# First layer of a two-layer decoder trunk: convolution over all 512 tokens at once, and Strassen's algorithm for nine of its FFN pairs

## The chip, the cores and the metric

The kernel runs on one core of one Trainium2 chip. The core has a matrix engine (TensorE, PE; its weight loads are listed as PEld), a vector engine (VectorE, DVE), a scalar engine (ScalarE, ACT), a general-purpose engine (GpSimd, POOL) and a queue that issues DMA transfers (SyncE, SP). Matmuls write PSUM, which has eight banks of 128 x 512 float32; all else lives in SBUF. The metric is the device time of one execution in microseconds (us).

## What is computed

Two layers over 512 tokens of width 1024, in float32. Layer 0 is a causal Conformer convolution followed by a SwiGLU FFN of hidden width 2816; layer 1 is sliding-window attention followed by another FFN. Only layer 0 and its neighbours matter here:

```python
def swiglu_ffn(x, w_up, w_down):
    gate, up = jnp.split(x @ w_up, 2, axis=-1)
    return (jax.nn.silu(gate) * up) @ w_down

def conformer_conv(x, w_pw1, b_pw1, w_dw, b_dw, ln_g, ln_b, w_pw2, b_pw2):
    a = jax.nn.glu(x @ w_pw1 + b_pw1, axis=-1)
    y = lax.conv_general_dilated(a, w_dw[:, None, :], window_strides=(1,),
        padding=((CONV_WIDTH - 1, 0),), feature_group_count=D_MODEL) + b_dw
    y = jax.nn.silu(layernorm(y, ln_g, ln_b))
    return y @ w_pw2 + b_pw2

# layer 0
h = h + conformer_conv(rmsnorm(h, norm_mix[0]), ...)
h = h + swiglu_ffn(rmsnorm(h, norm_ffn[0]), ffn_w_up[0], ffn_w_down[0])
# layer 1: K/V and queries from h, attention, output projection, FFN, final RMSNorm
```

The convolution is depthwise: each of 1024 channels has its own 31 taps along the tokens. The LayerNorm behind it runs over the channels, so it needs all channels of a token before any of them can go on.

## The kernel before

Activations are held transposed: channels on the 128 partitions, tokens along the free dimension, eight channel blocks (`KT`) of 128. `h` is the residual stream.

**Number formats on PE.** A float32 matmul (both operands float32) is recorded as two PE records. Most products instead split each operand into a high and a low part of a reduced format (float32r) and add three matmuls (`mm3`, L308 to L310); the split of a weight chunk is a cast on ACT (L249) and a subtraction on DVE (L250), done by `advance` some chunks ahead of use. Weights stream in chunks of 512 KB through one list, `PLAN`, by SP.

**Layer 0 is done in two halves of 256 tokens.** `Pw1` (line 778) is the first pointwise projection in float32, one channel block and half at a time, and `gate` makes the GLU into a padded row `a_pad`. `Half.taps` is the depthwise convolution of a block: `N_POOL` of the 31 taps are products on ACT (L817, L819) summed on POOL (L820); the others are multiply-adds on DVE into half a PSUM bank (L825, L827); POOL adds the two sums (L831). `conv` takes the blocks in pairs and alternates between the two. The LayerNorm statistics come from matmuls with an all-ones matrix of 128 x 128 over 256 columns (L876, L870), `scales_a` and `scales_b` make them into a mean and a scale per token, `spread` broadcasts these over the partitions with a matmul, and `rows` applies them with silu. `shift_rows` keeps the values small before they are squared.

The first half's convolution (`h0`) runs beside the 16 block-and-half projections. The second half's (`h1`) is a list of background steps (`job`) that `pace` hands out between weight chunks, while PE does `pw2` and the first part of the FFN for the first half: `pw2(h0.z)` in float32 (L306, `NATIVE`), then `ffn_part(0, 0, ..., HALF[0])` with five of the eleven FFN pairs at 256 columns. A pair is 256 hidden channels: `ffn_up` makes gate and up, `down_group` adds its part of the down product. Then the same for the second half, with the low part of a product fused behind the high part (`twin`, `mm2`, L340 and L341), reading the same weights from memory again. The other six pairs then run once over all 512 tokens (`ALL`).

**Layer 1's FFN** takes its first two pairs plainly at 512 columns, and the other nine by `ffn_prod`: one level of Strassen's algorithm, in which the product of a weight matrix cut in 2 x 2 blocks and an activation cut in 2 x 2 blocks takes seven block products in place of eight. The seven right factors are made once by `right_factors` in the background of the first part; the left ones are sums of weight blocks, made on DVE by `block` (L210 to L215) as the weights come in. The parts are `HALVES1` and `LAST`.

**Order.** Each engine takes its instructions in the order that the framework laid down when the kernel was built: instructions written earlier come first, but one that is not ready by the framework's own estimate is passed by a later one that is. `tc.issue_after` pins single instructions behind another. So the order in the code is a priority, not a promise.

Of the kernel before, what the change touches and what calls it, by code (L numbers as in the profile page):

```python
# [51 lines left out]
def chunk_plan():  # L52
# [7 lines left out]
    def ups(layer, lo, hi):  # L60
        for pair in range(lo, hi):
            if layer == 1 and pair >= PLAIN1:
                plan.extend(("prod", pair, j) for j in range(7))
# [11 lines left out]
    for _ in range(2):  # L75
        pw2()
        ffn(0, *HALVES0[0])
    ffn(0, *HALVES0[1])
# [20 lines left out]
NATIVE = {i for i in range(PLAN.index(("up", 0, 0, 0, 0)))}  # L99
CHUNKS = [("pw1", w * KT + ct) for ct in range(KT) for w in range(2)]  # L100
CHUNKS += [c for c in dict.fromkeys(PLAN) if c[0] != "prod"]
CHUNKS += [("up", 1, pair, half, which) for pair in range(PLAIN1, LAST[1]) for which in range(2) for half in range(2)]
# [3 lines left out]
def lay_weights(w):  # L106
# [3 lines left out]
    for i, c in enumerate(CHUNKS):  # L110
        if c[0] == "pw1":
            t = w["conv_w_pw1"][0][:, c[1] * P:(c[1] + 1) * P].reshape(KT, P, P)
# [44 lines left out]
def hybrid_trunk(ctx: ExitStack, tc: tile.TileContext, xT, W, prm_in, wdw_in, sinks, relb, onehot, fin, out):  # L157
# [35 lines left out]
    def load_block(i):  # L193
        _, pair, j = PLAN[i]
        if j == 0:
            four[pair] = str_pool[0].tile([P, 3, 1024], F32, tag="blocks", name=uid("blocks"))
        if j < 2:
            r = raws[i] = wpool.tile([P, 1024], F32, tag="raw", name=uid("raw"), bufs=4)
            nc.sync.dma_start(r, W[CHUNK_AT["up", 1, pair, j, 0]])
            nc.sync.dma_start(four[pair][:, j], W[CHUNK_AT["up", 1, pair, j, 1]])  # L200

    def block(i):

        _, pair, j = PLAN[i]
        b21, b22, s1 = (four[pair][:, n] for n in range(3))
# [29 lines left out]
    def advance():  # L235
        u = stream["use"]
        load(u + DMA_AHEAD)
        while stream["split"] < min(len(PLAN), u + SPLIT_AHEAD):
# [5 lines left out]
            if i in NATIVE:  # L244
                splits[i] = (r, None)
                continue
# [43 lines left out]
    def get(*key):  # L290
# [11 lines left out]
        return tuple(w and w.rearrange("p (a b) -> p a b", **sh) for w in (hi, lo))  # L302

    def mm3(out, w, x, start, stop, **kw):
        if w[1] is None:
            nc.tensor.matmul(out, w[0], x, start=start, stop=stop)  # L306
            return
# [4 lines left out]
    class Act:  # L312
        def __init__(self, n, w=512):
            self.per = 2048 // w
            self.q = [tuple(quads.tile([P, self.per, w], F32R, tag="quad", name=uid("quad")) for _ in range(2))
                      for _ in range(-(-n // self.per))]

        def __getitem__(self, i):
            a, b = self.q[i // self.per]
            return a[:, i % self.per, :], b[:, i % self.per, :]  # L320

    class Pairs:

        def __init__(self, n, w=512):
            self.per = 1024 // w
            self.q = [quads.tile([P, self.per, 2, w], F32R, tag="quad", name=uid("quad")) for _ in range(-(-n // self.per))]

        def both(self, i):
            return self.q[i // self.per][:, i % self.per]

        def __getitem__(self, i):
            b = self.both(i)
            return b[:, 0, :], b[:, 1, :]

    def mm2(out, w, x, start, stop):

        first, second = (w[0], x, out), (w[1], x[:, 0, :], out[:, 0, :])
        if stop:
            first, second = second, first
        nc.tensor.matmul(first[2], first[0], first[1], start=start, stop=False)  # L340
        nc.tensor.matmul(second[2], second[0], second[1], start=False, stop=stop)  # L341


    ALL = slice(0, S)
# [7 lines left out]
    w1 = [quads.tile([P, 2, KT, P], F32, tag="quad", name=uid("w1")) for _ in range(KT)]  # L352

    def load_x(tok):
        for i in range(0, KT, 2):
# [1031 lines left out]
```

## Time and the profile before

| | us |
|---|---|
| time, median of 3 runs | 1077.8 (1077.49 to 1079.34) |
| time of the profiled execution | 1077.63 |
| its span, first to last instruction | 1075.9 |
| first matmul of pw2, first half | 130.33 |
| first matmul of layer 1's FFN | 719.32 |

The profile lists busy time by engine, and in 40 equal slices of the span one digit each (9 is 90% or more). "Chain" is the work that ended last, followed back to what released it. Groups of instructions are given as line, engine, operation, result<-operands with shapes, count, then busy us and mean ns of one, then the idle time ahead of them and what ended it. A row of busy time by stage reads: stretch in us, its length, then busy us and count of instructions for PE, PEld, DVE, ACT and POOL, then the granted PE clock as a share of full speed, the share of time that the DMA engines were busy, and GB/s. A row of the timeline reads: start, duration, engine, line, operation, operands, count merged, and in brackets the idle time before it with what ended it. A row of the chain has start, duration and what ran. Durations of matmuls overlap, so paces are read from starts.

### The profile page before, as it was taken

How to read it: one execution, taken by the hardware profiler on the slowest of the kernel's cores; microseconds unless marked ns; L12 is line 12 of the kernel's file. 1: busy time of each engine (PE TensorE's matmuls, PEld its weight loads, DVE VectorE, ACT ScalarE, POOL GpSimd, SP SyncE). 2: the span in 40 equal slices, each digit the busy share in tenths (PEclk: the TensorE clock that was granted, in tenths of full speed). 3: DMA queues.
4: the chain of work that ended last, by engine and by line, in shares of the span. 5: the costliest groups of instructions: out<-in, count | busy, mean ns of one | idle time of the engine just before them, and what ended most of it. 6: DMA issues, size and time to landing. Idle time of an engine off the chain costs nothing.

```text
span 1075.9 us, 16385 instructions
## 1 busy us (share of the span) xinstructions
PE 1062.2 (99%) x6256; PEld 936.6 (87%) x6256; DVE 742.9 (69%) x1156; ACT 543.2 (50%) x959; POOL 307.2 (29%) x412
## 2 busy tenths in 40 slices
PE   9999998999999999999999999999999999999997
PEld 8888888999988888888888878788899988998996
DVE  3999989877777744444537576676978755776663
ACT  3887888754665423332325566453446522552353
POOL 3999999720231211111102244132100000000000
PEclk9999998999999999999999999999999999999999
DMA  9318045586556533332322211132423341243112
GB/s 358 121 20 98 3 144 170 159 260 188 177 177 196 176 98 98 98 98 99 98 98 79 79 59 41 49 108 79 157 79 99 101 158 56 85 138 111 40 60 79
DMA packets 39562, 123.45 MB, mean 115 GB/s; under 512 B 4251, under 2 KB 11068, under 8 KB 39484
## 3 DMA queue, kind: packets, MB, share of 16 engines
q1 hardware_dynamic: 38476, 121.19, 36.5%
q10 hardware_dynamic: 1008, 1.23, 0.3%
q8 instruction: 49, 0.80, 0.3%
q14 instruction: 29, 0.24, 0.1%
HBM read 117.15 MB, written 5.24 MB: 114 GB/s over the span
## 4 chain that ended last, share of the span: by engine, by line
PE 86%; DVE 6%; issue 3%; ACT 3%; POOL 1%; DMA 1%; POOLq 0%; SPq 0%; DVEq 0%
PE bank L308 18%; PE bank L309 18%; PE bank L310 18%; PE bank L1134 12%; PE bank L778 9%; PE bank L340 5%; PE bank L341 3%; DVE bank L827 2%; PE bank L1317 2%; DVE wlo L250 1%; DVE quad L450 1%; ACT pr L819 1%; POOL pr L820 1%; PE bank L876 1%; ACT z L921 0%
## 5 line engine op out<-in xcount | busy, mean ns | idle before, releaser
L309 PE MATMUL bank<-quad,whi 128*128 128x256 f32 (+1 forms) x1320 | 428.6, 326 | 2.5 <-DVE quad L450 2.5
L308 PE MATMUL bank<-quad,whi 128*128 128x256 f32 (+1 forms) x1320 | 427.5, 326 | 0.0
L310 PE MATMUL bank<-quad,wlo 128*128 128x256 f32 (+1 forms) x1320 | 425.3, 325 | 2.3 <-DVE wlo L250 2.3
L250 DVE TENSOR_TENSOR wlo<-raw,whi 128x1024 fp32r<-128x1024 f32 x190 | 255.0, 1343 | 181.0 <-ACT whi L249 176.8
L249 ACT CAST whi<-raw 128x1024 fp32r<-128x1024 f32 x190 | 199.2, 1049 | 286.2 <-PE bank L309 197.7
L309 PEld LDWEIGHTS bank<-quad,whi 128*128 128x128 f32 x1320 | 252.1, 191 | 24.2 <-DVE quad L450 3.8
L310 PEld LDWEIGHTS bank<-quad,wlo 128*128 128x128 f32 x1320 | 251.1, 191 | 22.8 <-DVE wlo L250 2.7
L308 PEld LDWEIGHTS bank<-quad,whi 128*128 128x128 f32 x1320 | 251.5, 191 | 20.9 <-issue 0.2
L820 POOL TENSOR_TENSOR pr<-pr,pr 128x256 f32<-128x256 f32 x208 | 158.3, 815 | 1.5 <-ACT pr L819 1.5
L778 PE MATMUL bank<-quad,w 128*128 128x256 f32 x512 | 114.6, 384 | 0.7 <-DMA w<-in_W_dram 0.7
L827 DVE SCALAR_TENSOR_TENSOR bank<-apad,wdw,bank 128x256 f32<-128x256 f32 x248 | 112.7, 484 | 3.4
L778 PEld LDWEIGHTS bank<-quad,w 128*128 128x128 f32 x512 | 98.4, 193 | 15.0 <-DVE quad L753 1.0
L819 ACT ACTIVATE pr<-apad,wdw 128x256 f32<-128x256 f32 x208 | 99.2, 502 | 20.6 <-POOL pr L820 18.7
L1328 POOL TENSOR_TENSOR rs<-ss,mhalf 128x1 f32<-128x1 f32 x4 | 2.2, 549 | 297.6 <-DVE ss L1326 297.6
L407 POOL TENSOR_TENSOR tmp<-tmp,tmp 128x256 f32<-128x256 f32 (+1 forms) x35 | 37.6, 1075 | 158.3 <-ACT tmp L403 121.5
L1134 PE MATMUL bank<-quad,whi 128*128 128x512 f32 x256 | 79.9, 393 | 0.0
L340 PE MATMUL bank<-quad,whi 128*128 128x512 f32 x212 | 75.9, 398 | 0.0
L579 POOL TENSOR_TENSOR tmp<-tmp,tmp 128x512 f32<-128x512 f32 x16 | 24.2, 1514 | 143.6 <-DVE tmp L578 143.6
L341 PE MATMUL bank<-quad,wlo 128*128 128x256 f32 x212 | 59.3, 280 | 0.0
L1134 PEld LDWEIGHTS bank<-quad,whi 128*128 128x128 f32 x256 | 47.2, 188 | 9.8 <-issue 0.4
L250 DVE TENSOR_TENSOR wlo<-blocks,whi 128x1024 fp32r<-128x1024 f32 x27 | 32.7, 1221 | 28.3 <-ACT whi L249 28.3
L249 ACT CAST whi<-blocks 128x1024 fp32r<-128x1024 f32 x27 | 28.3, 1048 | 45.8 <-PE bank L309 35.4
(186 smaller groups left out, 1202.6 us busy)
## 6 DMA issues: line engine op xcount, KB each, us to landing
raw<-in_W_dram SPq DMA_DIRECT2D x180, 512.0 KB, 3.6
blocks<-in_W_dram SPq DMA_DIRECT2D x18, 512.0 KB, 4.4
w<-in_W_dram SPq DMA_DIRECT2D x15, 512.0 KB, 9.7
fd<-fs SPq DMA_DIRECT2D x1, 3072.0 KB, 33.9
h<-in_xT_dram SPq DMA_DIRECT2D x8, 256.0 KB, 6.2
bias<-fd SPq DMA_DIRECT2D x8, 256.0 KB, 6.0
out_dram<-hg SPq DMA_DIRECT2D x3, 256.0 KB, 2.0
out_dram<-hg ACTq DMA_DIRECT2D x3, 256.0 KB, 2.4
```

Source lines behind the costliest of these rows:

```text
L249: nc.scalar.copy(hi, r)
L250: lo_engine[0].tensor_sub(lo, r, f32(hi))
L308: nc.tensor.matmul(out, w[0], x[0], start=start, stop=False, **kw)
L309: nc.tensor.matmul(out, w[0], x[1], start=False, stop=False, **kw)
L310: nc.tensor.matmul(out, w[1], x[0], start=False, stop=stop, **kw)
L340: nc.tensor.matmul(first[2], first[0], first[1], start=start, stop=False)
L341: nc.tensor.matmul(second[2], second[0], second[1], start=False, stop=stop)
L778: mm = nc.tensor.matmul(self.pb[:, w * W2:(w + 1) * W2], w1[ct][:, w, k, :], x[k] if x else xg[k][:, tok], start=k == 0, stop=k == KT - 1)
L819: on_act = nc.scalar.mul(pr, a[:, j:j + W2], tap(j))
L820: on_pool = nc.gpsimd.tensor_add(pr, acc, pr)
L827: on_dve = nc.vector.scalar_tensor_tensor(yt if i == nd - 1 else c, src, tap(i), c if i else self.shift, op0=ALU.mult, op1=ALU.add)
L1134: turn[0] = nc.tensor.matmul(*args, **kw).ins
```

## The change

Layer 0 is no longer cut in halves, and all but two of its FFN pairs go by Strassen's algorithm.

- `Pw1` handles all 512 tokens of a channel block: 16 float32 matmuls of 512 columns into two banks (`lin`, `gt`), the gate's matmuls first. `load_w1` brings a block's weights in one tile, ordered by input block; the first block's come on ACT's queue, in four pieces. There are at most five padded rows at a time.
- `Conv` does a block's taps at 512 columns, one chain a block, in a bank of its own. The split of the 31 taps is by block: `N_POOL` on ACT and POOL, `N_PE` on PE as matmuls with a diagonal matrix (`diagonal_taps`; the diagonals are products of the identity on ACT), the rest on DVE. `N_AHEAD` says how many steps of the tap stream are written ahead of each block's gate.
- The statistics (`sums`) are matmuls with the data as the weights and one column of ones, 128 tokens at a time; `scales` makes mean and scale.
- `pw2` runs once over 512 tokens with split operands.
- The FFN runs in four parts (`HALVES0`): pairs 0 and 1 plainly, then nine pairs by `ffn_prod`. `ffn_parts` is shared by both layers. `Pairs`, `mm2`, `twin`, the halves and the pinned background steps are gone.

```diff
-HALVES0 = ((0, 5), (5, 11))
+HALVES0 = ((0, 2), (2, 5), (5, 8), (8, 11))
-PLAIN1 = 2
+PLAIN = (2, 2)
-N_POOL = ((13, 13, 12, 12), (17, 15, 15, 15))
+N_POOL = (11, 11, 11, 11, 11, 11, 9, 7)
+N_PE = (0, 0, 0, 0, 0, 0, 7, 10)
+N_AHEAD = (0, 8, 17, 17, 17, 17, 17, 17)
...
-    for _ in range(2):
-        pw2()
-        ffn(0, *HALVES0[0])
-    ffn(0, *HALVES0[1])
+    pw2()
+    for part in HALVES0:
+        ffn(0, *part)
...
+    load_w1(0, ((0, 1), (1, 2), (2, 4), (4, 8)), nc.scalar)
+    for i in range(KT):
+        nc.sync.dma_start(hT[:, i, :], xT[i])
     nc.scalar.dma_start(wdw, wdw_in)
-    load_x(HALF[1])
     load_w1(1)
+    load_w1(2)
...
+        class Pw1:
+            def __init__(self, ct, x):
+                self.ct = ct
+                self.lin, self.gt = bank(), bank()
+                order = [(k, w) for w in (1, 0) for k in range(KT)]
+                if ct == 0:
+                    order = [(k, w) for k in range(KT) for w in (1, 0)]
+                for k, w in order:
+                    self.last = nc.tensor.matmul((self.lin, self.gt)[w], w1[ct][:, k, w, :], x[k],
+                                                 start=k == 0, stop=k == KT - 1).ins
...
+            def diagonal_taps(self):
+                if not self.n_pe:
+                    return
+                a = a_pad[self.ct]
+                self.pe = bank()
+                for n in range(self.n_pe):
+                    j = TAPS - self.n_pe + n
+                    dg = cv.tile([P, P], F32, tag="dg", name=uid("dg"), bufs=6)
+                    nc.scalar.mul(dg, ident, self.tap(j))
+                    nc.tensor.matmul(self.pe, dg, a[:, j:j + S], start=n == 0, stop=n == self.n_pe - 1)
+
+            def taps(self):
+                ct, nd, n_pool = self.ct, self.nd, self.n_pool
+                a, yt, tap = a_pad[ct], y[ct], self.tap
+                c = bank()
+                acc, pi = None, 0
+                for i in range(nd):
+                    while pi * nd < n_pool * (i + 1):
+                        j = nd + pi
+                        pr = cv.tile([P, S], F32, tag="pr", name=uid("pr"), bufs=6)
+                        if acc is None:
+                            nc.scalar.activation(pr, a[:, j:j + S], AF.Identity, scale=tap(j), bias=col("bdw", ct))
+                        else:
+                            nc.scalar.mul(pr, a[:, j:j + S], tap(j))
+                            nc.gpsimd.tensor_add(pr, acc, pr)
+                        acc = pr
+                        pi += 1
+                    src = a[:, i:i + S]
+                    if i == 0 and ct < 4:
+                        nc.vector.tensor_scalar(c, src, tap(i), None, op0=ALU.mult)
+                    else:
+                        nc.vector.scalar_tensor_tensor(yt if i == nd - 1 else c, src, tap(i), c if i else Conv.shift,
+                                                       op0=ALU.mult, op1=ALU.add)
+                    yield
+                if self.pe is not None:
+                    nc.vector.tensor_add(yt, self.pe, yt)
+                nc.gpsimd.tensor_add(yt, yt, acc)
...
+        def sums(ct):
+            nonlocal st
+            if ct < 4:
+                nc.vector.tensor_add(y[ct], y[ct], Conv.shift)
+            sq = cv.tile([P, S], F32, tag="sq", name=uid("sq"), bufs=2)
+            nc.scalar.square(sq, y[ct])
+            if st is None:
+                st = bank()
+            for f, t in enumerate((y[ct], sq)):
+                for n in range(NBLK):
+                    nc.tensor.matmul(st[:, f * NBLK + n:f * NBLK + n + 1], t[:, n * P:(n + 1) * P], ones_c,
+                                     start=sums_done[0] == 0, stop=sums_done[0] == 2 * KT * NBLK - 1)
+                    sums_done[0] += 1
+
+        def scales():
+            mv = small.tile([P, 4], F32, tag="mv", name=uid("mv"))
+            nc.vector.tensor_scalar(mv, st[:, 0:4], 1.0 / D, None, op0=ALU.mult)
+            dm = diagonals(mv)
+            pm = spread(dm)
...
+            nc.gpsimd.tensor_tensor(rr, var, mhalf, op=ALU.pow)
+            pr = spread(diagonals(rr))
+            return pm, pr
...
+        for ct in range(1, KT):
+            if ct + 1 < KT and ct > 1:
+                load_w1(ct + 1)
+            proj = Pw1(ct, xg)
+            run(N_AHEAD[ct])
+            convs[ct - 1].diagonal_taps()
+            proj.gate()
+            if ct == 3:
+                table_in()
+            if ct == 5:
+                table()
+        convs[KT - 1].diagonal_taps()
+        for _ in stream_taps:
+            pass
+        pm, prs = scales()
+        advance()
+        z = Act(KT)
+        for i in range(KT):
+            t = temp()
+            nc.vector.tensor_sub(t, y[i], pm)
+            nc.vector.tensor_mul(t, t, prs)
+            nc.scalar.activation(t, t, AF.Silu, scale=col("lng", i), bias=col("lnb", i))
+            split(z[i], t)
...
+    def ffn_parts(layer, parts, n, on_h=None):
+        gain = n.gains[0]
+        right = {}
+        background.append(factors(gain, n, right))
+        rate[0] = 1.5
+        ffn_part(layer, 0, n.x[gain], n.rms)
+        flush()
+        rate[0] = 0
+        for part in range(1, parts):
+            ffn_part(layer, part, right, None, on_h if part == parts - 1 else None)
+        return right
+
+    n0 = Next(("ffn0",))
+    pw2(z, n0)
+    nxt = Next(("kv", "mix1"))
     if True:
-        ffn_part(0, 1, x0["ffn0"], ALL, Both(), nxt.on_h)
+        ffn_parts(0, 4, n0, nxt.on_h)
```

The tap stream (`run`) goes block by block and appends `shift_rows` and `sums` as blocks are finished.

More of the change, by code (lines that the diff above doesn't have):

```diff
@@ L61, in ups @@
         for pair in range(lo, hi):
[L62 to L63 removed]
+            if pair >= PLAIN[layer]:
+                plan.extend(("prod", layer, pair, j) for j in range(7))
                 continue
@@ L1059, in hybrid_trunk, with all_taps @@
-        flush()
+        pb = spread(rms0.diag)
+        for i in range(KT):
+            nc.vector.scalar_tensor_tensor(xg[i], h[i], col("mix0", i), pb, op0=ALU.mult, op1=ALU.mult)
+        nc.scalar.copy(rms0.bc, pb)
+        first.gate(rms0.bc)
+        convs = [Conv(ct) for ct in range(KT)]
+        def all_taps():
+            for ct, c in enumerate(convs):
+                yield from c.taps()
+                if ct == 1:
+                    shift_rows()
+                    sums(0)
+                if ct >= 1:
+                    sums(ct)
```

659 lines of the change are left out of this document (148 added, 511 removed).

## The prediction

> **What bounds the kernel now.** I read the page's busy shares and slices first, then the chain that ended last, then the busy time by stage.
>
> ```profile
> span 1075.9 us, 16385 instructions
> PE 1062.2 (99%) x6256; PEld 936.6 (87%) x6256; DVE 742.9 (69%) x1156; ACT 543.2 (50%) x959; POOL 307.2 (29%) x412
> PE   9999998999999999999999999999999999999997
> DVE  3999989877777744444537576676978755776663
> POOL 3999999720231211111102244132100000000000
> PE 86%; DVE 6%; issue 3%; ACT 3%; POOL 1%; DMA 1%; POOLq 0%; SPq 0%; DVEq 0%
> 22.00:130.30 108.30, 108.30 (x505) 94.15 (x504) 101.42 (x242) 86.53 (x192) 104.47 (x152) 1.00 0.38 78
> 130.30:565.20 434.90, 429.84 (x2428) 378.94 (x2428) 281.89 (x378) 215.69 (x347) 134.10 (x139) 0.99 0.46 144
> 166.00:178.00 12.00, 8.64 (x45) 7.64 (x44) 12.00 (x17) 10.08 (x22) 12.00 (x14) 0.72 0.26 89
> ```
>
> The reader is to see that PE has work nearly all the time and makes up 86% of the chain, so time is won only by giving PE less to do, and lost wherever PE has to wait. While the first half's convolution runs (22 to 130 us) PE, DVE and POOL are all full: PE can only stay full there because it has the second half's projections to do. The second half's convolution lies beside PE's work on the first half.
>
> The span and the time of this execution, 1077.6 us, differ by 1.7 us, which the change leaves alone; the median shown, 1077.8 us, is 0.2 us above it.
>
> **The price of layer 0 behind the convolution.** The layer-1 FFN already runs in the changed form, so its stages can be moved over whole. The rows are starts of matmuls (and of one DVE add), time and duration in us.
>
> ```profile
> 130.33 0.44 PE L306 MATMUL bank<-z,raw 128*128 128x256 f32 x1
> 565.17 0.68 DVE L537 TENSOR_TENSOR h<-bank,h 128x512 f32<-128x512 f32 x1
> 719.32 0.39 PE L308 MATMUL bank<-quad,whi 128*128 128x512 f32 x1
> 786.43 0.28 PE L308 MATMUL bank<-quad,whi 128*128 128x256 f32 x1
> 910.89 0.28 PE L308 MATMUL bank<-quad,whi 128*128 128x256 f32 x1
> 1004.31 0.28 PE L308 MATMUL bank<-quad,whi 128*128 128x256 f32 x1
> 719.30:786.40 67.10, 67.10 (x299) 55.33 (x298) 57.71 (x62) 28.00 (x33) 12.00 (x7) 1.00 0.34 111
> 730.36 0.79 PE bank L417 x8
> 737.67 0.86 PE bank L442 x2
> ```
>
> Before, layer 0 takes from the first pw2 matmul (130.3) to the last residual add (565.2): 434.9 us. In layer 1 the first part (two plain pairs and their down products) runs from 719.3 to 786.4: 67.1 us, of which 0.79 and 0.86 are row statistics, so 288 matmuls of 512 columns take 65.5 us. The four Strassen pairs with their downs take 124.5 us (786.4 to 910.9), the next three 93.4 us (to 1004.3): 217.9/7 = 31.1 us a pair.
>
> After: pw2 is 192 such matmuls, 192/288 x 65.5 = 43.6; two plain pairs with statistics 67.1; nine Strassen pairs 9 x 31.1 = 280.1. **Sum 390.8, saving 44.1 us.** Strassen's own part is 9 x (65.5/2 - 31.1) = 14.6; the rest comes from work at 256 columns, from the statistics matmuls and from 5.1 us of idle PE (434.9 less 429.8) that go. The factors made in the background lie beside part 0 in layer 1 too, where PE was busy 67.1 of 67.1 us; without that cover DVE would hold PE up there, which is rival 3. Weights of pairs 0 to 4 are loaded once and not twice. The bias reads keep their place. The end, the K/V start and layer 1 are as before.
>
> So with T the time when pw2 can run, changed time = 1077.6 + (T - 130.3) - 44.1, and **even is T = 174.4**.
>
> **The price of the front.** What was hidden is now exposed: pw2 needs all eight channel blocks of all 512 tokens.
>
> ```profile
> 5.07 9.16 PE L778 MATMUL bank<-quad,w 128*128 128x256 f32 x32 [0.71 <-DMA w<-in_W_dram]
> 14.07 0.50 PE L417 MATMUL bank<-ones_c,tmp 128*128 128x1 f32 x4
> 14.61 0.16 DVE L419 TENSOR_SCALAR ms<-bank 128x2 f32<-128x2 f32 x1 [4.84 <-PE bank L417]
> 74.78 13.81 PE bank L778 x64
> 72.11 0.75 PE bank L976 x2
> L421 POOL TENSOR_TENSOR rs<-ms,mhalf 128x4 f32<-128x4 f32 x2 | 3.0, 1494 | 10.9 <-DVE ms L419 10.9
> L424 DVE TENSOR_TENSOR tmp<-ident,rs 128x512 f32<-128x512 f32 x2 | 1.4, 688 | 0.9 <-POOL rs L421 0.9
> L577 ACT ACTIVATE tmp<-tmp 128x512 f32<-128x512 f32 x16 | 10.1, 632 | 36.3 <-DVE tmp L576 36.3
> L403 ACT ACTIVATE tmp<-h 128x512 f32<-128x512 f32 x16 | 9.9, 617 | 0.0
> L453 ACT CAST quad<-tmp 128x512 fp32r<-128x512 f32 x42 | 25.5, 620 | 14.7 <-POOL tmp L579 10.8 <-DVE tmp L1156 2.6 <-DVE tmp L686 1.4
> ```
>
> *Start.* 64 records (32 fp32 matmuls of 256 columns) take 13.81, so 16 matmuls of 512 take 13.8 too. The first 32 records took 9.0 where 6.9 is the full rate: 2.1 us of start-up. The first projection then ends at 5.1 + 13.8 + 2.1 = 21.0; x and the weight pieces (now on ACT's queue, ahead of work that waits for x anyway) land under it. Row sums 0.8, mean 0.2, power 1.5, diagonal 0.7, spread 0.9 and some 0.4 of hand-overs: 25.5. One scaled row (0.7) on, at 26.2, the second projection starts; DVE does the other seven and the gate, and the first padded block is ready near 33.
>
> *PE from 26.2:* seven projections 96.7; shift 1.7; table 0.8; 17 diagonal taps of 512 columns at 0.86, 14.6; column sums of seven blocks at 8 x 0.20 (eight records are four matmuls, 0.79), 11.1. Sum 124.9, so **PE ends at 151.1** if it never waits.
>
> ```profile
> 38.54 5.96 DVE L827 SCALAR_TENSOR_TENSOR bank<-apad,wdw,bank 128x256 f32<-128x256 f32 x15
> 105.10 6.78 DVE L827 SCALAR_TENSOR_TENSOR bank<-apad,wdw,bank 128x256 f32<-128x256 f32 x13
> L827 DVE SCALAR_TENSOR_TENSOR bank<-apad,wdw,bank 128x256 f32<-128x256 f32 x248 | 112.7, 484 | 3.4
> L644 DVE SCALAR_TENSOR_TENSOR blocks<-h,prm,rsbc 128x512 f32<-128x512 f32 x8 | 5.5, 744 | 0.3 <-ACT rsbc L436 0.3
> 32.25 14.46 POOL L820 TENSOR_TENSOR pr<-pr,pr 128x256 f32<-128x256 f32 x21
> L579 POOL TENSOR_TENSOR tmp<-tmp,tmp x16: 1292/1437/2280, 388.8 to 769.9; 128x512 f32<-128x512 f32 x16
> L407 POOL TENSOR_TENSOR tmp<-tmp,tmp 128x512 f32<-128x512 f32 x14 | 21.7, 1549 | 93.4 <-ACT tmp L403 66.0 <-issue 26.2 <-POOL tmp L407 0.9
> L449 ACT ACTIVATE quad<-h,prm 128x512 fp32r<-128x512 f32 x24 | 16.5, 713 | 10.8 <-DVE h L1269 7.0 <-DVE h L537 3.8
> fd<-fs SPq DMA_DIRECT2D x1, 3072.0 KB, 33.9
> ```
>
> *DVE:* 149 taps of 512 columns (20 for six blocks, 15, 14). A 256 tap lasts 0.484 but comes at two paces: every 0.39 (15 in 5.96) and every 0.52 (13 in 6.78). I read the fast one as two chains taking turns in two banks, the slow one as one chain waiting for itself. By the 512 row (0.744, 0.26 more) a wide tap costs 0.65 or 0.78. With the 13 gates, shift and PE adds (0.66 each, 8.6) that is 105 or 125 us, and at the 94% that DVE reached in the 22 to 130 us stage, 112 or 133: end at 145 or 166. I take the fast end, because when DVE falls behind, the next block is there to take turns with.
>
> *POOL:* 82 adds. At 256 columns 21 came in 14.46, 0.69 each, as fast as its undisturbed 256 ones; so taps do not disturb it and I take the undisturbed 512 add, 1.29 less that overlap, 1.26: 103 us, from 34.3 to about 137. At the disturbed mean of 1.55 it is 127 us, to 161. ACT has 82 products of at most 0.71 (58 us); its gates, squares and 17 small diagonals lie in what it has left of the 118 us from 33 to 151.
>
> *SP:* the bias table's write (33.9 us to landing) now stands ahead of the last projection weights and of the pw2 weights. It is a matter of the DMA engines, busy 0.38 in that stage, and the projections are in order: I take nothing, and a late weight would cost PE one projection's start.
>
> So PE is last, at 151.1, with the ten diagonal taps of block 7 (they need its gate). PE's sum is added on DVE (0.7), POOL adds its share (1.3), 1 us for waits: **the last block at 154**. Then a chain with nothing beside it: square 0.6, sums 0.8, four small DVE operations 0.6, diagonal 0.7, power 1.5, diagonal 0.7, spread 0.9, multiply 0.7, silu 0.6, copy 0.6, ten hand-overs at 0.15: 9.2, so first operand at 163.2. PE idles there, and idle cost clock before: the 166 to 178 us row shows a mean clock of 0.72, so 12 x 0.28 = 3.4 us lost. The low half of the first row is 0.7 later. Further rows come every 2.6 us on DVE (three operations and half a weight split), and PE uses one in 2.7, so that cover is thin but holds. **T = 167.3**, 7.1 us under even: 1070.5, I say 1071.
>
> The Trainium skill speaks against such a gap: "TensorE: Matmul & The Clock Gate", Part 1, says that a window of about 3.4 us without work halves the clock and that as long a busy window restores it. By that page the loss would be about 1.7 us (an estimate) and the time 1069; the trace's 3.4 us decides here.
>
> **Rivals.**
> 1. *POOL's adds stay disturbed* (1.55 each): last block at 161, T near 175, 1078 us, no change. For it: the 512 rows go up to 2.28. Against: those ran beside DVE work with two SBUF operands, the taps have one.
> 2. *Slower: one chain on DVE.* Banks are eight: two projections in flight hold four, sums and shift one each, a chain one, and one is left for a second chain or the diagonal taps. If chains do not take turns, a tap costs 0.78, DVE ends at 166, POOL's add and 0.7 later 168, T near 181: 1085 us. It turns slower from about 0.75 a tap ((149 x 0.75 + 8.6)/0.94 from 33 is 161, a last block at 163, 2 us past the 161.1 that is even). Against: the 15 taps in 5.96. [...]
> 3. *Strassen does not pay in layer 0* (DVE starves PE): 14.6 us back, 1085 us. Against: seven pairs in layer 1 without a PE wait.
>
> **How the numbers follow.** Forecast 0.68 (own range 1062 to 1076, from no waits and 1.7 us of clock loss to 4 us more of waits), rival 1 0.11, rival 2 0.16, rival 3 0.05. A measurement can tell about 0.2% (2 us) from no change. Faster: 0.66 of the forecast and 0.04 of rival 1: 0.70. Same: 0.02, 0.05 of rival 1, 0.03 of a mild rival 2: 0.10. Slower: 0.20. Range 1061 to 1084: it takes in rival 1 and the milder half of rival 2.
>
> **What would show it.** Right: first pw2 matmul near 163, PE full from 26 to about 150, POOL done with block 6 before that, pw2 to last residual add near 395 us, Strassen pairs at 31.1. Wrong: POOL adds over 1.5 us, long runs of taps every 0.78, PE waits among the projections (column sums queued ahead of data), z rows slower than 2.7 us, a clock below 1 for longer than 7 us.

## The result, and the profile after

| | before | after |
|---|---|---|
| time, median | 1077.74 us (4 runs) | 1091.8 us (1091.28 to 1095.16, 4 runs) |
| ratio, 95% interval | 1 | 1.0134 [1.0111, 1.0157] |
| span of the profiled execution | 1075.9 us | 1089.6 us |
| first matmul of pw2 | 130.33 us | 184.22 us |

The change is 14 us slower, where 7 us faster was forecast, and the time lies 8 us outside the range. The two halves of the forecast fared very differently. First the page of the changed kernel, with the slices of TensorE and its clock, and the busy time by stage:

```profile
span 1089.6 us, 15353 instructions
PE 1055.6 (97%) x6130; PEld 882.1 (81%) x6130; DVE 774.8 (71%) x1023; ACT 498.4 (46%) x768; POOL 205.4 (19%) x226
PE   6999986999999999999999999999999999999997
PEclk9899995999999999999999999999999999999999
```
```profile
31.30:166.00 134.70, 126.48 (x360) 61.43 (x360) 119.88 (x171) 70.97 (x110) 100.77 (x83) 0.97 0.31 63
166.00:184.20 18.20, 11.14 (x36) 7.91 (x36) 7.85 (x17) 4.50 (x7) 3.51 (x3) 0.50 0.37 115
184.20:297.20 113.00, 112.98 (x490) 93.07 (x491) 86.94 (x96) 49.21 (x64) 19.94 (x12) 0.98 0.30 94
297.20:390.60 93.40, 93.40 (x649) 87.59 (x649) 65.91 (x70) 39.36 (x48) 0.00 (x0) 1.00 0.34 108
390.60:484.10 93.50, 93.50 (x650) 87.64 (x650) 64.78 (x68) 39.35 (x48) 0.00 (x0) 1.00 0.33 102
```

**Behind the convolution the forecast held.** Three Strassen pairs take 93.4 us, 31.1 a pair, with TensorE busy throughout. From the first pw2 matmul to the K/V matmul that waits for VectorE is 589.02 - 184.22 = 404.8 us; before, the same stretch was 575.54 - 130.33 = 445.2. That is 40.4 us saved; the forecast had 44.1 less 3.4 of clock and 0.7 for the low half, 40.0. The two rows, before and after:

```profile
575.54 0.50 PE L309 MATMUL bank<-quad,whi 128*128 128x512 f32 x1 [0.87 <-DVE quad L450]
```
```profile
589.02 0.50 PE L304 MATMUL bank<-quad,whi 128*128 128x512 f32 x1 [0.91 <-DVE quad L408]
```

**The whole miss is in the front.** The first pw2 matmul was expected at 163.2 (9.2 behind 154) and came at 184.2, 21.0 later. The timeline of the changed kernel, TensorE's rows, then VectorE's, then GpSimd's (start, duration, what; in brackets the idle time before it and what ended it):

```profile
18.88 0.95 PE L377 MATMUL bank<-ones_c,tmp 128*128 128x1 f32 x8
28.40 2.08 PE L400 MATMUL bank<-tmp,ones_m 128*128 128x512 f32 x2 [8.57 <-DVE tmp L393]
31.32 43.53 PE L631 MATMUL bank<-quad,w 128*128 128x512 f32 x96 [0.84 <-DVE quad L743]
...
157.86 0.72 PE L715 MATMUL bank<-ones_c,sq 128*128 128x1 f32 x6
168.89 1.87 PE L715 MATMUL bank<-ones_c,quad 128*128 128x1 f32 x8 [10.31 <-POOL quad L697]
...
174.04 1.84 PE L715 MATMUL bank<-ones_c,sq 128*128 128x1 f32 x8
176.86 2.08 PE L400 MATMUL bank<-tmp,ones_m 128*128 128x512 f32 x2 [0.98 <-DVE tmp L393]
179.17 2.08 PE L400 MATMUL bank<-tmp,ones_m 128*128 128x512 f32 x2 [0.23 <-DVE tmp L393]
184.22 2.08 PE L303 MATMUL bank<-quad,whi 128*128 128x512 f32 x4 [2.97 <-ACT quad L411]
```
```profile
21.43 5.00 DVE L248 TENSOR_TENSOR wlo<-raw,whi 128x1024 fp32r<-128x1024 f32 x4 [6.96 <-ACT whi L247]
26.36 0.16 DVE L379 TENSOR_SCALAR ms<-bank 128x4 f32<-128x4 f32 x1
...
49.90 10.62 DVE L692 SCALAR_TENSOR_TENSOR bank<-apad,wdw,bank 128x512 f32<-128x512 f32 x16
...
74.95 0.75 DVE L645 SCALAR_TENSOR_TENSOR apad<-bank,prm,tmp 128x512 f32<-128x512 f32 x1 [4.68 <-PE bank L631]
...
78.59 14.21 DVE L692 SCALAR_TENSOR_TENSOR bank<-apad,wdw,bank 128x512 f32<-128x512 f32 x18
...
115.16 0.69 DVE L708 TENSOR_TENSOR quad<-quad,bank 128x512 f32<-128x512 f32 x1 [2.45 <-POOL quad L697]
...
165.53 1.28 DVE L696 TENSOR_TENSOR quad<-bank,quad 128x512 f32<-128x512 f32 x2
```
```profile
166.36 2.48 POOL L697 TENSOR_TENSOR quad<-quad,pr 128x512 f32<-128x512 f32 x2 [14.01 <-DVE quad L696]
```

Three pieces make up the 21.0 us:

- *Start, 5.1.* The second projection starts at 31.3, not 26.2. The row sums were done at 19.8, but `ms` stands in VectorE's queue behind four weight subtractions for pw2, whose casts waited for weights from memory. Nothing needs those weights before 184.
- *Convolution, 9.7.* Its last add ends at 168.8 (154 + 5.1 = 159.1 was due). TensorE is done at 158.6; VectorE at 166.8. Taps come every 0.66 us where two chains take turns (16 in 10.62) and every 0.79 where one chain waits for itself (18 in 14.21); counted from the starts of successive taps, 73 steps are of the second kind and 65 of the first, so single chains cost some 9 us. VectorE also waits 10 us between 31 and 167 for the projections behind its gates, for the shift rows and for GpSimd. GpSimd itself idles 14 us ahead of its last adds.
- *Tail, 6.2.* From 168.8 to the first pw2 matmul is 15.4 us, where 9.2 was priced. The last two blocks end together, so the sums of both are on the path, and TensorE runs them, both spreads and the head of pw2 at half clock (0.50 in that stage; the granted clock is at half from 161.8 to 189.1).

### The profile page after: what moved, and what is told of

It reads as the page before. It is cut to its first block, busy times and chain, and to the rows that moved or that the text cites. A ratio compares the mean times of both kernels' runs of the same rounds, so it can differ in the third digit from the quotient of the medians.

```text
span 1089.6 us, 15353 instructions
## 1 busy us (share of the span) xinstructions
PE 1055.6 (97%) x6130; PEld 882.1 (81%) x6130; DVE 774.8 (71%) x1023; ACT 498.4 (46%) x768; POOL 205.4 (19%) x226
## 4 chain that ended last, share of the span: by engine, by line
PE 91%; DVE 4%; DMA 2%; issue 1%; ACT 1%; POOL 0%; POOLq 0%; ACTq 0%; DVEq 0%
PE bank L303 22%; PE bank L304 22%; PE bank L305 22%; PE bank L887 12%; PE bank L631 9%; DVE bank L692 2%; PE bank L1057 2%; PE bank L715 1%; DVE quad L408 1%; DMA raw<-in_W_dram 1%; DMA h<-in_xT_dram 1%; DMA w<-in_W_dram 1%; DVE wlo L248 0%; PE bank L400 0%; DMA prm<-in_prm_dram 0%
## 5 line engine op out<-in xcount | busy, mean ns | idle before, releaser
L304 PE MATMUL bank<-quad,whi 128*128 128x256 f32 (+1 forms) x1536 | 490.2, 321 | 0.9 <-DVE quad L408 0.9
L303 PE MATMUL bank<-quad,whi 128*128 128x256 f32 (+1 forms) x1536 | 485.7, 321 | 3.3 <-ACT quad L411 3.0
L305 PE MATMUL bank<-quad,wlo 128*128 128x256 f32 (+1 forms) x1536 | 483.0, 320 | 0.0
L303 PEld LDWEIGHTS bank<-quad,whi 128*128 128x128 f32 x1536 | 291.7, 191 | 26.8 <-ACT quad L411 4.5
L304 PEld LDWEIGHTS bank<-quad,whi 128*128 128x128 f32 x1536 | 293.1, 191 | 22.9 <-DVE quad L408 1.3
L248 DVE TENSOR_TENSOR wlo<-raw,whi 128x1024 fp32r<-128x1024 f32 x160 | 199.4, 1247 | 114.6 <-ACT whi L247 106.8
L631 PE MATMUL bank<-quad,w 128*128 128x512 f32 x256 | 113.4, 603 | 1.6 <-DVE quad L743 0.8
L692 DVE SCALAR_TENSOR_TENSOR bank<-apad,wdw,bank 128x512 f32<-128x512 f32 x137 | 98.1, 753 | 2.5
L685 POOL TENSOR_TENSOR pr<-pr,pr 128x512 f32<-128x512 f32 x74 | 93.5, 1272 | 24.0 <-ACT pr L684 20.1
L887 PE MATMUL bank<-quad,whi 128*128 128x512 f32 x256 | 79.9, 393 | 0.0
L684 ACT ACTIVATE pr<-apad,wdw 128x512 f32<-128x512 f32 x74 | 51.6, 717 | 21.4 <-POOL pr L685 20.1
L887 PEld LDWEIGHTS bank<-quad,whi 128*128 128x128 f32 x256 | 47.2, 188 | 9.8 <-issue 0.4
L887 PE MATMUL bank<-quad,wlo 128*128 128x512 f32 x128 | 49.9, 390 | 0.0
```

Of the source, the lines that this page charges most:

```text
L248: lo_engine[0].tensor_sub(lo, r, f32(hi))
L303: nc.tensor.matmul(out, w[0], x[0], start=start, stop=False, **kw)
L304: nc.tensor.matmul(out, w[0], x[1], start=False, stop=False, **kw)
L305: nc.tensor.matmul(out, w[1], x[0], start=False, stop=stop, **kw)
L631: self.last = nc.tensor.matmul((self.lin, self.gt)[w], w1[ct][:, k, w, :], x[k], start=k == 0, stop=k == KT - 1).ins
L684: nc.scalar.mul(pr, a[:, j:j + S], tap(j))
```

## The experiments

Times are medians; beside them the kernel before took 1077.3 to 1078.2 us. "The last add" below means the end of the last GpSimd add, which completes the convolution.

### Undoing one suspected cost at a time

**Subtractions later.** The four subtractions are pinned behind the convolution's last VectorE adds, the casts behind a copy:

```diff
-            nc.scalar.copy(hi, r)
-            lo_engine[0].tensor_sub(lo, r, f32(hi))
+            with ExitStack() as es:
+                for ins in pins if i < 4 else ():
+                    es.enter_context(tc.issue_after(ins))
+                nc.scalar.copy(hi, r)
+                lo_engine[0].tensor_sub(lo, r, f32(hi))
...
+        pins.append(nc.scalar.copy(rms0.bc, pb).ins)
...
+        pins[1:] = Conv.added
```

> The four weight splits of pw2 that stand ahead of the RMS mean on DVE are queued behind the convolution's last DVE adds instead. Theory (they held the front up: the mean came at 26.4 where the row sums were done at 19.7): the second projection starts 5 us earlier (near 26), and as PE and DVE work without long waits from there, pw2 starts 5 us earlier: 1086 to 1088 us. Rival (the early start is lost again in waits of DVE's fixed order between the blocks): the second projection starts near 26, pw2 starts within 2 us of 184, time 1090 to 1092.

1090.92 us, ratio 1.0125 [1.0106, 1.0144]: 0.9 us gained in the median, within the noise (the four executions go from 1088.0 to 1092.9). VectorE's rows, with `ms` first:

```profile
19.85 0.16 DVE L383 TENSOR_SCALAR ms<-bank 128x4 f32<-128x4 f32 x1 [5.65 <-PE bank L381]
...
34.90 0.75 DVE L649 SCALAR_TENSOR_TENSOR apad<-bank,prm,tmp 128x512 f32<-128x512 f32 x1 [4.52 <-ACT tmp L647]
...
109.39 0.69 DVE L713 TENSOR_TENSOR quad<-quad,bank 128x512 f32<-128x512 f32 x1 [2.91 <-POOL quad L702]
```

`ms` runs 6.5 us earlier, but the moved casts now stand ahead of the first gate's sigmoid on ScalarE (4.5 us), and waits between fixed positions swallow part of the rest (5.5 us for GpSimd, 4.0 for gates). The time is the rival's; in the profiled execution, the lowest of the four, the first pw2 matmul comes at 181.6, 2.6 earlier than in the changed kernel, between the two expectations.

**Fewer taps on VectorE.** `N_POOL` of blocks 6 and 7 from (9, 7) to (11, 11).

> Blocks 6 and 7 take 11 taps each on ACT and POOL (9 and 7 in the changed kernel), so DVE has six taps fewer, POOL six adds more. Theory (DVE's taps set when the last block is done, at 0.66 us a tap): last block and pw2 4 us earlier, 1088 us. Rival (PE's diagonal taps and the sums behind them set it): no change, 1092. Second rival (POOL becomes last, 1.26 an add): 1091 or more.

1087.7 us, ratio 1.0088 [1.0073, 1.0103]: 4.1 us for six taps, 0.68 each, as expected. VectorE's work does set the end there: the last two blocks' sums start at 164.5 instead of 168.9.

**Constant matmuls against the clock.** 45 float32 matmuls of 128 columns (two records each) behind the last diagonal tap.

> 45 matmuls of 128 columns on constants are put on PE behind the last diagonal tap, to keep it at work for 10 us; the column sums of blocks 6 and 7 are queued behind them. Theory (the tail is long because PE sits idle and its clock is at half: the sums of two blocks took 6.9 us, each spread 2.1, and pw2 began at half clock): sums 3.4 to 4, spreads 1.1, granted clock near 1 when pw2 begins, 6 to 8 us in all, 1084 to 1086. Rival (the tail's length is hand-overs between engines): sums faster, but not more than 2 us in all, 1090.

1090.46 us, ratio 1.0117 [1.0102, 1.0132]. TensorE's rows:

```profile
158.25 10.21 PE L780 MATMUL bank<-ones_m 128*128 128x128 f32 x90
168.29 0.50 PE L716 MATMUL bank<-ones_c,sq 128*128 128x1 f32 x4
169.33 1.05 PE L716 MATMUL bank<-ones_c,quad 128*128 128x1 f32 x8 [0.53 <-POOL quad L697]
...
172.04 1.85 PE L716 MATMUL bank<-ones_c,sq 128*128 128x1 f32 x8
174.87 2.08 PE L400 MATMUL bank<-tmp,ones_m 128*128 128x512 f32 x2 [0.98 <-DVE tmp L393]
```

The sums run at 0.13 us each and fall back to 0.23 some 4 us after the dense stretch: sums alone do not hold the clock. The gain is 1.3 us, nearer the rival.

**No Strassen in layer 0.** All eleven pairs plain.

> All eleven pairs of layer 0 go plainly at 512 columns in the same four parts, and no right factors are made there; the front is unchanged. Theory (a Strassen pair with its downs costs 31.1 us and a plain one 32.7, in layer 0 as in layer 1): 14.6 us slower than the changed kernel, 1106. Rival (layer 0 loses Strassen's gain to DVE or to waits): 1092 to 1098.

1104.75 us, ratio 1.0250 [1.0234, 1.0265]: 13.0 us slower than the changed kernel, where 14.6 was the price (1106 expected). Strassen's part is not the fault.

### Is it the pace of single chains?

Each block's taps go in turns into two banks; GpSimd joins them.

```diff
-                c = bank()
+                c2 = (bank(), bank())
...
+                    c = c2[i % 2]
...
+                nc.gpsimd.tensor_add(acc, acc, half)
                 nc.gpsimd.tensor_add(yt, yt, acc)
```

> Each block's VectorE taps go in turns into two banks instead of one, and GpSimd adds the second sum (8 adds more). Nothing else is changed. Theory (VectorE's pace): in the changed kernel some 60 to 75 of the 149 taps stand in a single chain and come every 0.79 us, the others every 0.66; with two chains all come at 0.66, 8 to 10 us less on VectorE, its last tap at 156 to 158 instead of 165.5; TensorE's diagonal taps end at 158.6, so of that 7 or so is gained: 1084 to 1086. Rival (VectorE's waits for gates and banks set its end, not the pace): the taps come at 0.66 and the time won is waited away; last tap at 163 or later, 1089 to 1092.

> The two chains, and 11 taps on GpSimd in blocks 6 and 7 instead of 9 and 7 (6 taps fewer on VectorE). Theory: both gains add up as far as TensorE's 158.6 lets them, 1081 to 1085. Rival: TensorE's end or GpSimd's (96 adds of 1.26 are 121 us from 33 on, 154) is the bound, and nothing comes on top of the two chains alone: within 1 us of that run.

> As the run before, and the four subtractions of pw2's weight splits behind the last VectorE add of the convolution, as in the first experiment. Theory: TensorE and VectorE both start 5 to 7 us earlier; with the pace no longer lost to single chains the start now reaches the end: 5 to 7 us below the run before, 1074 to 1080, about the kernel before (1078). Rival (as in the first experiment, waits in VectorE's fixed order eat it): 1 to 3 us below the run before, 1079 to 1083.

1089.55, 1091.02 and 1090.89 us (ratios 1.0112, 1.0124, 1.0118, each about 0.002 either way). Three relieving edits together give next to nothing. The first is as its rival said, and so is the second within the noise: the six taps fewer that gave 4.1 us alone give nothing here. The third fits neither of its expectations. In the first, taps come at 0.66 throughout, as meant, and VectorE's rows show where the time goes:

```profile
66.69 0.75 DVE L694 SCALAR_TENSOR_TENSOR quad<-apad,wdw,bank 128x512 f32<-128x512 f32 x1
74.80 0.75 DVE L645 SCALAR_TENSOR_TENSOR apad<-bank,prm,tmp 128x512 f32<-128x512 f32 x1 [7.36 <-PE bank L631]
78.22 1.28 DVE L711 TENSOR_TENSOR quad<-quad,bank 128x512 f32<-128x512 f32 x2 [2.67 <-PE bank L706]
```

Blocks 0 and 1 are finished at 67.4; the next thing in VectorE's queue is gate 3, whose projection ends at 74.7, although block 2's padded row had been ready since 62.8. In the third of these runs TensorE is caught as well; its shift matmul waits for GpSimd, with the next projection queued behind it:

```profile
73.89 2.08 PE L711 MATMUL bank<-quad,inv_s 128*128 128x512 f32 x2 [4.80 <-POOL quad L705]
```

So faster taps arrive early at the same fixed meeting points. In the first of these runs no step of 0.79 is left, which is worth some 9 us, yet VectorE's last tap ends only 1.8 us earlier (163.8 instead of 165.6); its waits for gates grew from 5.7 to 10.6 us, for GpSimd from 3.4 to 5.0, and for the shift from 0.9 to 2.7. A part of the last two can be the joining adds, which these runs give to GpSimd on top; the wait for gate 3 is TensorE's alone. The theory of the pace fell; the order became the suspect.

### A new order

Casts behind gate 6's sigmoid; the shift taken from block 0 alone and kept in SBUF; a block's shift add and sums written 10 taps into the next block; more taps ahead of each gate; 11 GpSimd taps in every block.

```diff
-N_AHEAD = (0, 8, 17, 17, 17, 17, 17, 17)
+N_AHEAD = (0, 10, 20, 20, 20, 20, 20, 20)
...
-                yield from c.taps()
-                if ct == 1:
-                    shift_rows()
-                    sums(0)
-                if ct >= 1:
-                    sums(ct)
+                for i, _ in enumerate(c.taps()):
+                    if ct >= 1 and i == min(16 if ct == 1 else 10, c.nd - 1):
+                        if ct == 1:
+                            shift_rows()
+                        sums(ct - 1)
+                    yield
+            sums(KT - 1)
```

> One chain per block again, but the order of VectorE laid down anew: the four weight subtractions behind the convolution's last add and ScalarE's four casts behind the sigmoid of gate 6; 11 GpSimd taps in every block; the statistics' shift from block 0 alone, kept in SBUF; each block's shift add and sums 10 taps into the next block; 10 taps ahead of gate 1 and 20 more ahead of each later gate instead of 8 and 17. In this order VectorE's taps alternate between two blocks nearly throughout. Theory (the fixed order and the single chains cost VectorE its fast pace, its waits then cost TensorE): second projection at 24, VectorE's and TensorE's work for the convolution end at 153 to 157 instead of 166.8 and 158.6; then two adds, sums, spreads as before, first pw2 matmul at 172 to 176 instead of 184.2: 1080 to 1084. Rival (TensorE's or GpSimd's own work is the bound, whatever the order): the convolution ends at 162 or later, 1087 to 1090.

> The run before and 35 constant matmuls (128 columns) behind the last diagonal tap, ahead of the last block's sums. Theory: the last sums run at 0.13 us each instead of 0.23, 2 to 3 us less than the run before. Rival: the clock falls during the sums anyway, as in the filler run: 1 us or less.

> As the reordered run, but with two chains per block and 10 GpSimd taps instead of 11 (GpSimd has 10 adds, the joining add and the last: 12 or 13 of 1.26 per block, as in the reordered run). 8 taps more on VectorE. Theory: within 2 us of the reordered run, since there the taps alternate already; rival (waiting on the joining add): 3 to 6 us slower than that run.

**1079.79 us**, ratio 1.0026 [1.0016, 1.0037], 12 us better than the changed kernel. With the constant matmuls 1083.65: 70 records took 8 us and held the last sums back by 5, too many; neither expectation holds. With two chains 1083.86, 4 us slower, as the rival said: the joining add lengthens GpSimd (its last add ends at 166.3).

The profiled execution of the reordered run is the longest of its ten, 1084.07 us at a granted clock of 0.939. The run with 35 constant matmuls has the same order at 0.986, and its trace agrees on what follows (last add at 163.3, where the first has 164.2; 7.5 us of waits for diagonals, where the first has 8.1).

Now TensorE worked without a gap from 76 us to its last diagonal tap, and VectorE waited for its diagonals. So: 5 and 7 of those instead of 7 and 10, sums of blocks 0 and 1 later, 12 constant matmuls; then two chains in block 7.

> The reordered run with 5 and 7 diagonal taps on TensorE in blocks 6 and 7 instead of 7 and 10 (5 taps more on VectorE), the sums of blocks 0 and 1 behind the fourth projection's matmuls (TensorE stood 2.5 us there for VectorE and ran at half clock for some us after), and 12 constant matmuls ahead of the last block's sums. Theory (in the reordered run TensorE is the bound: it works without a gap from 76 to 162, while VectorE waits 8 us for diagonal taps): TensorE is 4.5 us shorter and loses 3 to 5 us less to the wait; the last sums start at 158 to 160 instead of 164.2, first pw2 matmul at 169 to 172: 1072 to 1076, faster than the kernel before. Rival (VectorE, with the last block in one chain behind gate 7, is late instead): the last add at 161 or later as before, 1077 to 1080.

> The run before with two chains in the last block alone (GpSimd joins them). Theory: its 13 taps come at 0.66 instead of 0.79, 1.5 us less at the end: 1 to 2 us below the run before. Rival: the last block doesn't wait for VectorE, within 0.7 us of it.

1079.7 and 1082.56 us. The first misses its 1072 to 1076: no gain in the median, although the last add came at 158.4 instead of 163.3 in the profiled execution, which, at 1077.5, was among the lowest of eleven. The second adds an operation to GpSimd, whose end went to 162.3; it is 2.9 us slower than the first, which neither expectation has. VectorE still stood at the head of block 7's taps, in the first of them:

```profile
138.97 0.75 DVE L651 SCALAR_TENSOR_TENSOR apad<-bank,prm,tmp 128x512 f32<-128x512 f32 x1
143.83 0.69 DVE L703 TENSOR_TENSOR quad<-bank,quad 128x512 f32<-128x512 f32 x1 [4.11 <-PE bank L677]
```

The add of block 6's diagonal sum, pinned behind the first eight taps of block 7 (the expectation says nine), takes that wait away:

> As the run with 5 and 7 diagonal taps, but without the constant matmuls; the add of block 6's diagonal sum stands behind nine taps of block 7 on VectorE instead of ahead of them (VectorE stood 4.1 us there for TensorE), and on ScalarE each cast stands ahead of the next silu. Theory (the order laid down on VectorE still costs its last block 4 us): the last add ends at 153 to 154 instead of 156.1, the last block's sums start at 154 to 156 instead of 158.4 and run at full clock (0.13 us each, 2 us together instead of 3.6), the first cast is 0.7 earlier; first pw2 matmul at 163 to 166 instead of 170.4: 1072 to 1075, faster than the kernel before. Rival: TensorE's last diagonal tap (152) and the adds behind it hold the end: last sums at 157 or later, 1077 to 1079, no faster than the kernel before.

1080.28 us, ratio 1.0027 [1.0018, 1.0037]: no gain, a miss again. VectorE's last add ended 4 us earlier, and GpSimd's rows show what had been hidden beside it:

```profile
149.07 8.36 POOL L693 TENSOR_TENSOR pr<-pr,pr 128x512 f32<-128x512 f32 x5
157.52 2.12 POOL L713 TENSOR_TENSOR quad<-quad,pr 128x512 f32<-128x512 f32 x1
```

Singly, three of the five adds take 1.27 us, as usual; the other two and the last take 2.12, and they lie beside VectorE's weight subtractions, which take 2.1 to 2.3 there and 1.2 alone. So GpSimd gets fewer taps: (10, 8), or (11, 8) with 8 diagonals in block 7.

> The run before with 10 and 8 GpSimd taps in blocks 6 and 7 instead of 11 and 11 (4 taps more on VectorE, 2.6 us). In the run before, VectorE's last add ended at 152.1 and TensorE's diagonals at 151.4, but GpSimd's adds of the last block at 157.5 and its final one at 159.6 (five adds at 1.67 instead of 1.26, beside the four weight subtractions). Theory (GpSimd was the last of three engines that are now level): VectorE's last add at 154 to 155, GpSimd's final one at 156 instead of 159.6, the sums right behind TensorE's work and so nearer full clock: 3 to 6 us less, 1074 to 1077. Rival: VectorE is now as late as GpSimd was, 1079 to 1081.

> As the run beside it, with 11 and 8 GpSimd taps and 5 and 8 diagonal taps (1 tap more on VectorE, 1 more on TensorE, 3 fewer on GpSimd than in the run with the last block first). Theory: TensorE 0.9 us longer (152.3), VectorE's last add at 153, GpSimd's final one at 155 to 156: 1073 to 1077, level with or below the run beside it. Rival: 1079 to 1081.

1076.05 us, ratio 0.9986 [0.9977, 0.9995], and **1075.53 us, ratio 0.9982 [0.9973, 0.9991]**, the best of all and just below the kernel before. Both are as expected. The last one, VectorE then GpSimd then TensorE:

```profile
153.41 0.69 DVE L712 TENSOR_TENSOR quad<-bank,quad 128x512 f32<-128x512 f32 x1
```
```profile
154.25 2.11 POOL L713 TENSOR_TENSOR quad<-quad,pr 128x512 f32<-128x512 f32 x1 [1.76 <-DVE quad L712]
```
```profile
148.65 1.96 PE L678 MATMUL bank<-apad,dg 128*128 128x512 f32 x4
...
156.41 1.86 PE L733 MATMUL bank<-ones_c,quad 128*128 128x1 f32 x8 [4.12 <-POOL quad L713]
...
167.75 2.08 PE L307 MATMUL bank<-quad,whi 128*128 128x512 f32 x4 [2.41 <-ACT quad L415]
```

TensorE's diagonals end at 150.6, VectorE at 154.1 and GpSimd at 156.4; the first pw2 matmul is at 167.8.

### Order or split?

That run changes both the order and the split of the taps. Each alone, in the changed kernel:

> The changed kernel with nothing but the fastest run's split of the taps: 11 and 8 on GpSimd and 5 and 8 as diagonals in blocks 6 and 7 (instead of 9 and 7, 7 and 10). VectorE has 150 taps instead of 149, TensorE 4 diagonal taps fewer. Theory (the order is the cause, the split only lets it pay): VectorE is still last and has one tap more, so no gain: 1090 to 1093. Rival (the split alone, by its relief of TensorE, is the gain): 1084 or less.

> The fastest run with the changed kernel's split of the taps (9 and 7 on GpSimd, 7 and 10 as diagonals): the new order alone. Theory: most of the 16 us stays, less what TensorE's four diagonal taps more cost at its end (4 x 0.92, 3.7 us): 1078 to 1081. Rival (the split is the gain): 1086 or more.

The split alone: 1091.29 us, ratio 1.0136 [1.0120, 1.0152], the same as the changed kernel. The order alone (with the shift from block 0, and each cast ahead of the next silu): **1077.74 us**, ratio 1.0007 [0.9998, 1.0017], a little below the 1078 to 1081 expected. So 14 of the 16 us are the order, and only then is the split worth 2. The same 14 us stand between the two traces. The rows of the order alone, TensorE's second projection, GpSimd's last add, the first pw2 matmul:

```profile
24.78 43.16 PE L636 MATMUL bank<-quad,w 128*128 128x512 f32 x96 [0.84 <-DVE quad L761]
```
```profile
156.68 2.11 POOL L713 TENSOR_TENSOR quad<-quad,pr 128x512 f32<-128x512 f32 x1 [6.40 <-DVE quad L712]
```
```profile
170.18 2.08 PE L307 MATMUL bank<-quad,whi 128*128 128x512 f32 x4 [2.41 <-ACT quad L415]
```

The start is 6.5 us earlier (24.8 for 31.3), the last add 10.0 (158.8 for 168.8), the first pw2 matmul 14.0 (170.2 for 184.2): 6.5 from the start, 3.5 within the convolution, 4.0 from the tail, where the sums of one block are left instead of two. The pace hardly changed: 59 steps of single chains instead of 73, some 2 us.

"The order" is a bundle: the late weight splits, the places of the sums and of block 6's last add, more taps ahead of each gate, the shift from one block, each cast ahead of the next silu. Only the late splits were run alone in the changed kernel; which of the others carries how much is not tested. The shift in SBUF also frees a PSUM bank. No wait of TensorE or VectorE between 31 and 158 us in the changed kernel's trace ends with a bank becoming free, so this is an unlikely cause, but it was not tested alone.

The table of what VectorE waited for, first the changed kernel (31 to 167 us), then the order alone (31 to 160):

```profile
DVE apad L645 <- PE bank L631: 5.7, 3, 4.7
DVE quad L708 <- POOL quad L697: 3.4, 2, 2.5
```
```profile
DVE quad L712 <- PE bank L678: 4.6, 2, 3.5
DVE apad L652 <- ACT tmp L650: 1.5, 1, 1.5
```

The waits for projections are gone and that for GpSimd is 0.3 us; what is left comes at the end and is TensorE's own work, but for the 1.5 us ahead of the first gate that both kernels have.

## Why the prediction was wrong

- *Layer 0 behind the convolution:* right, in mechanism and size (40.4 against 40.0; Strassen 31.1 a pair; 13.0 for Strassen where 14.6 was said).
- *Work of TensorE and GpSimd:* right. TensorE was busy 126.5 us in the convolution's stage (124.9 forecast), GpSimd's adds took 1.27 (1.26). Rival 1 does not hold for the changed kernel.
- *The step that failed* is "so PE is last, at 151.1", with "when DVE falls behind, the next block is there to take turns with". It summed each engine by itself, took the fast pace for all of VectorE's taps, put its end at 145, and took the largest sum. In the trace TensorE is done at 158.6 and VectorE, the last, at 166.8. The engines meet at several places in a block (gate, shift add, last add, sums), at positions laid down when the kernel was built, and an engine that comes early does not go on to ready work behind such a position: in the run with two chains VectorE stood 7.4 us ahead of gate 3 with block 2's taps ready. The forecast's own front said that the order "is a priority, not a promise", and then priced none of it. VectorE's end, at 166.8, is the 166 of rival 2 only by luck: rival 2 has all taps in single chains and no late start, the trace has half of them so, a start 5.1 us late and 10 us of waits. With the pace put right (two chains) the median moved 2.3 us; with the order put right, and the pace nearly as before, 14.
- *The start* failed in the same way: the time between row sums and `ms` was priced by its operations (0.2), and nobody asked what stands ahead of `ms` in VectorE's queue. It cost 5.1 us; a repair of this alone moved the median by 0.9 us. That the next meeting points took the rest is read from one trace (4.5 us at the first gate, 5.5 for GpSimd).
- *The tail* was mis-sized, 15.4 for 9.2. Half of one block's sums at full clock were priced (0.8, the half behind the square; the forecast's own price of a block is 1.6); two blocks' sums at half clock stand there, 7.0 us from 168.9 to 175.9. The lost clock was one term of 3.4 us behind the wait; in the trace the half clock falls on the sums, both spreads and the first 5 us of pw2. The Trainium skill, "TensorE: Matmul & The Clock Gate", Part 1, has the clock halve after some 3.4 us of idle and come back after as much work: the trace's two levels and the fall 4 us after the dense stretch agree, but the Trainium skill speaks of a window without work, and in the run with 35 constant matmuls the clock fell 2.2 us behind the last of them (at 170.3) while TensorE ran sums without a pause.

The limit is visible too. With order and split right, the first pw2 matmul is at 167.8, 4.6 behind the forecast's 163.2, and the time is 4.5 above 1071. In the best form that was found the change is worth about 2 us, not 7.

## What to carry to other kernels

When three engines are nearly level, the sum of each says little: list, for each in-order queue, what it must wait for and in which order, and ask at each such place which engine arrives first and what ready work lies behind it. Price a gap's first and last users, not just the gap: low-priority work that was written early can sit ahead of the one instruction that everything waits for. And a relieved wait that gave nothing here showed the next engine that was level: when VectorE's last wait was gone, GpSimd was last, and taking three or four taps from it brought the gain.

## What was not expected of the hardware

- Matmuls of one column do not keep the clock. In the run with 45 constant matmuls dense work ended at 168.5, and the sums behind it, with one pause of 0.5 us, ran at 0.13 us each and from 172.0 on at 0.23. The time to the fall differs from trace to trace: 2.2 us in the run with 35 of them.
- VectorE's operations with both operands in SBUF disturb GpSimd and are disturbed by it; its taps, with one in SBUF and one in PSUM, are not. In the reordered kernels the shift lies in SBUF; the view of that tile in the first of them (count, then shortest, median and longest duration in ns, first and last start) has

```profile
L699 DVE SCALAR_TENSOR_TENSOR bank<-apad,wdw,shift x5: 747/1109/1676, 77.5 to 144.2; 128x512 f32<-128x512 f32 x5
L717 DVE TENSOR_TENSOR quad<-quad,shift x3: 845/1755/1759, 74.4 to 109.6; 128x512 f32<-128x512 f32 x3
```

  against 0.75 and 0.69 us with the shift in PSUM, and GpSimd's last add beside the weight subtractions took 2.1 instead of 1.26. In the changed kernel, beside the taps, its 74 product adds took 1.26 to 1.28. The Trainium skill, "SBUF — State Buffer", section "Who interferes with whom", names a port pair that the two share and that one of them holds at a time; these rows agree. The waits that rival 1 feared exist, then, but the changed kernel avoids them by keeping its chains in PSUM.
- Taps that last 0.75 us come every 0.66 if they belong to two chains in two banks, and every 0.79 if to one.
